# Two trunk layers at fp32: the second and third quarter of the in-projection in one written order

## The chip, the cores and the metric

The kernel runs on one core of a Trainium2 chip. The metric is the device time of one execution in microseconds (us). An execution has one launch; all weights are read from the chip's memory (HBM) once, some 613 MB in all. Five engines work side by side, each in its own order of instructions: TensorE (PE, with its weight loads shown as PEld), VectorE (DVE), ScalarE (ACT), GpSimd (POOL) and SyncE (SP), whose queue issues the transfers. They wait for each other by semaphores.

## What is computed

One inference step of a trunk of two layers with model width 2048, for two groups of requests: 128 context tokens and 128 latent tokens. Everything is float32. Layer 0 mixes with latent attention and grouped-query attention side by side (one combined in-projection of 2048 x 2880, one out-projection), layer 1 with differential attention; each is followed by a gated feed-forward part with a width-3 convolution. Each of these four sub-layers has an adaptive norm:

```python
mod = jax.nn.silu(cond) @ w_ada[l] + b_ada[l]
sh1, sc1, gt1, sh2, sc2, gt2 = jnp.split(mod[:, None, :], 6, axis=-1)
h = rmsnorm(x, g_norm_mix[l]) * (1 + sc1) + sh1
...
proj = h @ w_in
...
x = x + gt1 * m
```

`cond` is one vector for the context group and one for the latent group, so `silu(cond) @ w_ada` is a product with two rows over a 2048 x 12288 matrix for each layer: some 200 MB of weights for very little arithmetic. These weights are a third of the traffic, and the kernel spreads their work over all stages.

## The kernel before

**Layout.** Features lie on the partitions, and both groups of tokens side by side as 256 columns. A matrix product in fp32 is made of three in the type fp32r: weights and activations are each split into a high and a low part, and `wh·xh`, `wh·xl`, `wl·xh` are summed. `split` (lines 243 to 245) does it: a cast on ScalarE writes the high part, a subtraction on VectorE the low part, which therefore comes later. All products go through the helper at line 104, all transposes through the one at line 107, so in the profile they are told apart by tiles: `acc` are the sums of the big products, `ada` those of the adaptive norm.

**Weights** (class `Weights`). A `raw` tile of 1 MB holds 16 blocks of 128 x 128; there are three such buffers, loaded by SyncE's queue (line 291). Its blocks are split eight at a time (1024 columns) into `wh` and `wl`, of which there are four buffers each. `ahead` splits one half of a tile ahead of its use, in pieces of 512 columns, and can be told to pin these instructions. `gemm` makes one output chunk of 128 features; sums have three buffers (`pacc`), and the next chunk can start while an earlier one is still read out.

**Order.** The program is written in one stream, and a planner orders each engine's instructions by a simulated timeline. Instructions handed to `keep_order` keep the program's order among each other on their engine. The object `pe` hands every TensorE instruction to it while `pe.in_turn` is set; before the change that was used in layer 1's mixer alone.

**The adaptive norm's rows.** Units of `w_ada` (layer, one of six parts j, quarter q of the features) are worked off in the order of the list `ROWS`. A unit is four tiles of 1 MB (`row_step`, load at line 534; `araw` with two buffers, for the first units every other tile in the weights' `raw` buffers). `sum_rows` multiplies each tile with `condw`, in four products. `ada_finish` then copies the sums to `am` on ScalarE (line 408), transposes them on TensorE and writes `mod` on VectorE (lines 424 and 426). The first quarter of layer 0 is cut into two halves (`load_half`, `half_unit`, line 359 and lines 363 to 379), so that the first products can start early. `ensure` runs a unit's remaining steps at once; `pump`, called after each chunk, runs as many steps as the stage's rate says.

Some units have no TensorE work for the rows: VectorE sums them in blocks of 256 KB (`side_step`, `sum_block`). A block is loaded at line 497 (three buffers) and takes two instructions at line 478 or 481, one per group, which are pinned. `SIDE` says how many blocks go with one chunk in each stage. A unit has 16 blocks and ends like the others, with a sum over partitions, a copy into `am` and a turn. Three such units (`BESIDE[0]`) belong to layer 0, six to layer 1. Their pool is `beside` in layer 0 and the mixer's own in layer 1. What follows in the pool's place has to wait until the blocks are done, among it `condb` (line 440), a load that lies on SyncE's queue near the end of layer 0's out-projection.

**The in-projection of layer 0** (`mixer_ab`). It is cut along the input features, because the adaptive norm's values come quarter by quarter. `modulate` (lines 591 to 606) makes `hx` for the chunks of a quarter: VectorE and ScalarE scale and shift, ScalarE casts the high part (606), VectorE or GpSimd subtract the low part. `part` then runs 23 output chunks over the quarter's input features: `act.copy` (843) writes the sum for the first part, `dve.tensor_tensor` (845) adds it for the others.

- First quarter: two halves of two input blocks each (6 products per chunk). Beside the first half lie the loads and sums of the second pair of half units (`second_half`).
- Second to fourth quarter: four input blocks each (12 products per chunk). Before each, `ensure` finishes that quarter's two units (scale and shift), then `modulate` runs, then `part`.
- With the fourth quarter `pinned[0]` is set, the caches are loaded, and the blocks on VectorE start (`side_start`). The finishing work of the columns (norms, rotary) runs beside it.

After that come the heads (`head_ab`; softmax weights `p`, line 713), the out-projection with 16 chunks of 48 products and the residual add on VectorE (line 656), and the feed-forward part.

Of the kernel before, what the change touches and what calls it, by code (L numbers as in the profile page):

```python
# [17 lines left out]
P = 128  # L18
D = 2048
KD = D // P  # L20
# [60 lines left out]
FLIMIT = {"ab": 0, "ffn0": 12, "c": 12, "ffn1": 15}  # L81

BESIDE = {0: [17, 18, 19], 1: [26, 27, 28, 29, 30, 31]}
SIDE = {"in3": 0.6, "heads": 1.05, "out0": 0.9, "c": 1.7, "outc": 2.0}
INV = {2048: 0, 768: 1, 512: 2, 128: 3, 256: 4}


# [1 line left out]
def step_kernel(ctx: ExitStack, tc: tile.TileContext, A: dict):  # L89
# [299 lines left out]
    def ada_finish(l, j, q, on_dve, acc=None):  # L389

        got = ada if not on_dve else dict(ada)
        if acc is not None:
            got["acc"] = acc
        home = bank if acc is not None else lambda: T_(ppool["ada"], [P, 512], "ada", bufs=1)

        def reduce():
            ps = home()
            for c in range(2):
                for h in range(2):
                    g = 2 * c + h  # L400
                    pe.matmul(ps[32 * g:32 * g + 32, :NT], C("pick"), got["acc"][c][:, h * NT:(h + 1) * NT],
                              start=True, stop=True, skip_group_check=True)
            got["ps"] = ps

        def copy():
            n = NT if on_dve else 512
            am = T_(tmp, [P, 512], "am", bufs=1)
            act.copy(am[:, :n], got["ps"][:, :n])
            got["am"] = am

        def turn(pin=None):
            pt = bank() if pin else home()
            pin = pin or (lambda i: i)
            for b in range(2 if on_dve else 4):
                pin(pe.transpose(pt[:, b * P:(b + 1) * P], got["am"][:, b * P:(b + 1) * P], ident))
            out = mod[:, l, j, 4 * q:4 * q + 4]
            bias = vector("bada", l, j, q)
            if on_dve:
                two = lambda v: v.rearrange("p (h b) c -> p b c h", b=2)
                dve.tensor_tensor(  # L420
                    out=two(out), in1=two(bias), op=ALU.add,
                    in0=pt[:, :NT].rearrange("p (b c h r) -> p b c h r", b=2, c=2, h=2)[:, :, :, :, 0])
            else:
                dve.tensor_reduce(out=out, in_=pt.rearrange("p (b g r) -> p b r g", b=4, g=4)[:, :, 0:2],
                                  axis=AX.X, op=ALU.add)
# [44 lines left out]
                keep_order(i)  # L470


    side = {"units": [], "k": 0, "due": 0.0, "rate": 0.0, "then": [], "apart": False}

    def sum_block(acc, block, k):
        for c in range(2):
            if k == 0:
                i = dve.tensor_scalar(out=acc[c], in0=block, scalar1=condw[:, k, c:c + 1],
                                      scalar2=None, op0=ALU.mult)
            else:  # L480
                i = dve.scalar_tensor_tensor(out=acc[c], in0=block, scalar=condw[:, k, c:c + 1],  # L481
                                             in1=acc[c], op0=ALU.mult, op1=ALU.add)
            keep_order(i)

    def side_step():
        if side["then"] and not side["apart"]:
# [6 lines left out]
        if k == 0:  # L493
            acc = T_(side["pool"], [P, 2, 512], "aacc", bufs=2 if side["apart"] else 1)
            side["acc"] = [acc[:, 0], acc[:, 1]]
        block = T_(side["pool"], [P, 512], "block", bufs=3)
        sp.dma_start(out=block, in_=A["w_ada"][u[0], u[1], u[2], k // 4][:, k % 4])
        sum_block(side["acc"], block, k)
        side["k"] = (k + 1) % KD
        if k == KD - 1:  # L500
            wait = [lambda: None] * 2 if side["apart"] else []
# [2 lines left out]

    def side_start(name, units, pool_, apart=False):

        side.update(units=[ROWS[u] for u in units], pool=pool_, rate=SIDE[name], due=0.0, apart=apart)

    def side_pump():
        if side["apart"] and side["then"]:  # L510
# [215 lines left out]
    def mixer_ab(hx, rb0, st, beside):  # L726
        l = 0
        with tc.tile_pool(name="ab", bufs=1) as ab:
            with tc.tile_pool(name="abp", bufs=1) as pj:
# [104 lines left out]
                    elif c == 15:  # L834
                        start(values(1))

                def part(W, k0, n, first, rate, between=None, **kw):

                    for c in range(23):
                        ps = gemm(W.chunk(), lambda k: hx[:, k0 + k, :NT], lambda k: hx[:, k0 + k, NT:2 * NT])  # L840
# [4 lines left out]
                            dve.tensor_tensor(out=to, in0=to, in1=ps, op=ALU.add)  # L845
                        if between:
                            between(c)
                        pump(rate, **kw)

                second = {}  # L850
# [10 lines left out]
                        pump(RATE["in0"], until=4)  # L861

                for h in range(2):
                    modulate(hx, rb0, 0, 0, range(2 * h, 2 * h + 2))
                    W = Weights(A["w_in_ab"][3 * h:3 * h + 3], 2, 8, cycle=23)
                    if h == 0:
                        part(W, 0, 2, True, 0, second_half)
                    else:
                        part(W, 2, 2, False, RATE["in0"], until=4)
                W = Weights(A["w_in_ab"][6:], 4, 4, cycle=23)  # L870
                for q in range(1, 4):
                    ensure(0, 1, [q])
# [483 lines left out]
```

## Time and profile before

| | |
|---|---|
| median of 3 runs | 2364.98 us (2364.43 to 2365.27) |
| profiled execution | 2362.85 us |
| its span (first to last instruction) | 2361.1 us |
| mean granted TensorE clock | 0.993 |
| moved by DMA | 612.96 MB, mean 260 GB/s |

The stretches that the change reaches, and what lies around them (bounds rounded to the stage's edges; busy time in us):

| us | stage | PE | DVE | ACT | granted clock | GB/s |
|---|---|---|---|---|---|---|
| 0 to 24 | first loads, first two half units | 9.11 | 8.52 | 9.39 | 1.00 | 366 |
| 24 to 60 | first quarter | 31.25 | 14.81 | 17.66 | 0.91 | 370 |
| 60 to 165 | second and third quarter | 99.78 | 60.10 | 33.66 | 0.98 | 334 |
| 165 to 240 | fourth quarter | 74.05 | 71.91 | 44.98 | 1.00 | 297 |
| 240 to 366 | heads | 124.17 | 88.02 | 63.56 | 1.00 | 308 |
| 366 to 460 | out-projection | 90.98 | 64.03 | 39.28 | 1.00 | 291 |
| 460 to 1160 | feed-forward of layer 0 | 697.16 | 641.91 | 357.12 | 1.00 | 267 |
| 1160 to 2361 | layer 1 | 1180.22 | 898.50 | 598.80 | 0.99 | 233 |

How such rows are read: an engine's busy time is the sum of its instructions' times, and register, branch and DMA-issuing instructions aren't counted. The granted clock is the TensorE clock that the throttle allowed, as a share of full speed. In the timelines quoted below a row gives the time from the span's start, the busy time, the engine, the line, the operation, the output and input tiles, the shapes and how many instructions the row groups; in square brackets stands how long the engine had waited before and for what. In rows of waits, the total, the number of waits and the longest follow the colon.

### The profile page before, as it was taken

What the parts mean: (1) busy time and instruction counts of PE and PEld (TensorE: products, weight loads), DVE (VectorE), ACT (ScalarE), POOL (GpSimd) and SP (SyncE); (2) the same over time, 40 slices, a digit from 0 to 9 for tenths busy, and PEclk for the clock granted to TensorE, in tenths of its full rate; (3) what the DMA queues carried; (4) which work ended last, traced back from release to release, by engine and by line L of the source; (5) the groups of instructions that cost most, each with busy time, mean ns of one, the idle gap of its engine ahead of it and who ended that gap; (6) DMA issues with size and microseconds to landing.
All of it is one profiled execution on the core that took longest, in us unless ns stands there. A gap on an engine that the chain in (4) does not pass through costs nothing. (4 is left out here: it accounts for less than half of the span.)

```text
span 2361.1 us, 47623 instructions
## 1 busy us (share of the span) xinstructions
PE 2306.7 (98%) x19624; PEld 2183.2 (92%) x19624; DVE 1847.8 (78%) x2822; ACT 1164.5 (49%) x1857; POOL 175.7 (7%) x210
## 2 busy tenths in 40 slices
PE   6999999999999999999999999999999999999997
PEld 4778768899999999999989999998999999999997
DVE  3569866779999999999878888798899755666654
ACT  4245544465553355554464444446555534555543
POOL 0002202100000000001220000022000000000011
PEclk9999999999999999999999999999999999999999
DMA  9988888667777877777768888777677555555553
GB/s 368 360 310 283 310 316 328 248 241 251 261 265 285 303 268 260 262 259 274 285 249 279 306 295 312 249 242 271 245 260 258 198 194 197 197 195 191 192 193 124
DMA packets 108249, 612.96 MB, mean 260 GB/s; under 512 B 11712, under 2 KB 19584, under 8 KB 40832
## 3 DMA queue, kind: packets, MB, share of 16 engines
q1 hardware_dynamic: 108032, 609.92, 71.3%
q8 instruction: 154, 2.52, 0.4%
q14 instruction: 63, 0.52, 0.1%
HBM read 605.12 MB, written 4.75 MB: 258 GB/s over the span
## 5 line engine op out<-in xcount | busy, mean ns | idle before, releaser
L104 PE MATMUL acc<-hx,wh 128*128 128x256 f32 x8416 | 1456.3, 278 | 9.3 <-ACT hx L606 4.4
L104 PEld LDWEIGHTS acc<-hx,wh 128*128 128x128 f32 x8416 | 1272.6, 188 | 46.8 <-issue 16.6
L244 ACT CAST wh<-raw 128x1024 fp32r<-128x1024 f32 (+1 forms) x822 | 795.3, 978 | 943.1 <-PE acc L104 759.7
L245 DVE TENSOR_TENSOR wl<-raw,wh 128x1024 fp32r<-128x1024 f32 (+1 forms) x822 | 923.8, 1141 | 315.6 <-ACT wh L244 310.4
L104 PE MATMUL acc<-hx,wl 128*128 128x256 f32 x4208 | 1167.6, 278 | 2.5 <-DVE wl L245 2.3
L104 PEld LDWEIGHTS acc<-hx,wl 128*128 128x128 f32 x4208 | 790.7, 188 | 20.1 <-issue 7.1
L104 PE MATMUL acc<-g,wh 128*128 128x256 f32 x2816 | 478.8, 276 | 0.0
L104 PEld LDWEIGHTS acc<-g,wh 128*128 128x128 f32 x2816 | 423.4, 188 | 0.0
L104 PE MATMUL acc<-g,wl 128*128 128x256 f32 x1408 | 388.0, 276 | 0.0
L452 DVE CUSTOM_DVE_ANT_0 junk<-araw,condb 128x2048 f32<-128x2048 f32 x120 | 274.7, 2289 | 0.0
L104 PEld LDWEIGHTS acc<-g,wl 128*128 128x128 f32 x1408 | 264.2, 188 | 0.0
L481 DVE SCALAR_TENSOR_TENSOR aacc<-block,condw,aacc 128x512 f32<-128x512 f32 x270 | 199.0, 769 | 9.3 <-DMA block<-w_ada 9.0
L200 POOL TENSOR_TENSOR sqacc<-sqacc,sq 128x256 f32<-128x256 f32 x62 | 91.3, 1472 | 1507.6 <-issue 1210.6
L1127 ACT ACTIVATE cv<-acc,convw 128x256 f32<-128x256 f32 x176 | 98.2, 558 | 5.1 <-PE acc L104 5.1
L104 PE MATMUL acc<-oall,wh 128*128 128x256 f32 x512 | 90.3, 281 | 1.8 <-DVE oall L245 1.1
L104 PE MATMUL ada<-araw,condw 128*32 128x512 f32 (+1 forms) x608 | 77.4, 591 | 13.6 <-DMA araw<-w_ada 13.0
L656 DVE SCALAR_TENSOR_TENSOR x<-acc,mod,x 128x128 f32<-128x128 f32 x192 | 58.1, 343 | 39.6 <-PE acc L104 39.6
L1130 DVE SCALAR_TENSOR_TENSOR cv<-acc,convw,cv 128x254 f32<-128x254 f32 x176 | 83.6, 475 | 6.1 <-ACT cv L1127 6.1
L1133 DVE SCALAR_TENSOR_TENSOR cv<-acc,convw,cv 128x254 f32<-128x254 f32 x176 | 84.4, 479 | 3.6
L104 PEld LDWEIGHTS acc<-oall,wh 128*128 128x128 f32 x512 | 78.4, 191 | 2.7 <-DVE oall L245 1.3
L104 PE MATMUL acc<-oall,wl 128*128 128x256 f32 x256 | 71.4, 280 | 0.0
L196 ACT ACTIVATE sq<-x 128x256 f32<-128x256 f32 x75 | 31.0, 415 | 36.2 <-DVE x L656 32.4
(194 smaller groups left out, 1273.7 us busy)
## 6 DMA issues: line engine op xcount, KB each, us to landing
raw<-w_up SPq DMA_DIRECT2D x176, 1024.0 KB, 4.8
araw<-w_ada SPq DMA_DIRECT2D x142, 1024.0 KB, 5.8
raw<-w_down SPq DMA_DIRECT2D x88, 1024.0 KB, 4.8
raw<-w_in_c SPq DMA_DIRECT2D x48, 1024.0 KB, 6.6
block<-w_ada SPq DMA_DIRECT2D x144, 256.0 KB, 5.2
raw<-w_in_ab SPq DMA_DIRECT2D x19, 1024.0 KB, 6.1
raw<-w_out_ab SPq DMA_DIRECT2D x16, 1024.0 KB, 7.4
raw<-w_out_c SPq DMA_DIRECT2D x16, 1024.0 KB, 6.9
```

The costliest lines, as they stand in the source:

```text
L104: return self.placed(nc.tensor.matmul(*a, **kw))
L196: act.activation(sq, src, AF.Square)
L200: eng.tensor_tensor(out=st["acc"], in0=st["acc"], in1=sq, op=ALU.add)
L244: pin(act.copy(out_hi, src))
L245: pin(dve.tensor_tensor(out=out_lo, in0=src, in1=out_hi.bitcast(F32), op=ALU.subtract))
L452: keep_order(dve.tensor_tensor_reduce(out=T_(feat["pool"], [P, D], "junk"), in1=feat["row"][:, c], in0=feat["raw"].rearrange("p g n -> p ( ...
L481: i = dve.scalar_tensor_tensor(out=acc[c], in0=block, scalar=condw[:, k, c:c + 1], in1=acc[c], op0=ALU.mult, op1=ALU.add)
L656: dve.scalar_tensor_tensor(out=x[:, c, s], in0=ps[:, s], scalar=mod[:, l, 3 * which + 2, c, g:g + 1], in1=x[:, c, s], op0=ALU.mult, op1=AL ...
L1127: pin(act.activation(y, ps, AF.Identity, scale=cw[:, 1, m:m + 1], bias=cw[:, 3, m:m + 1]))
L1130: pin(dve.scalar_tensor_tensor(out=y3[:, :, 1:], in0=p3[:, :, :T - 1], scalar=cw[:, 0, m:m + 1], in1=y3[:, :, 1:], op0=ALU.mult, op1=ALU.add))
L1133: pin(dve.scalar_tensor_tensor(out=y3[:, :, :T - 1], in0=p3[:, :, 1:], scalar=cw[:, 2, m:m + 1], in1=y3[:, :, :T - 1], op0=ALU.mult, op1=A ...
```

## The change

It has four parts.

1. **The first weights.** In `mixer_ab` the weights of each half of the first quarter are set up ahead of `modulate`, and for the first half `W.ahead(keep_order)` is called there: the first 8 blocks' splits are made in pieces of 512 columns, pinned. On ScalarE they so stand behind the pinned or earlier instructions of the program, the copy `am` of the second half unit among them.
2. **The blocks' loads.** `side_load` loads a block; `side_start` calls it twice with its issue pinned, and `side_step` then always loads two blocks ahead of the one it sums. As the loads are pinned on SyncE, the planner can't put the first of them at the program's start.
3. **The second and third quarter.** A function `rows(q)` finishes a quarter's two units and modulates. It is called for the second quarter ahead of the loop, and for the third and fourth inside `part`, after chunk 18 of 23 (counted from 0) of the quarter before, through the new argument `then`. During the second and third quarter `pe.in_turn` is set: TensorE's instructions keep the order in which they are written. In the fourth quarter it isn't.
4. **The rates.** `SIDE` rises from 0.6 to 0.7 blocks per chunk in the fourth quarter, from 1.05 to 1.15 in the heads, from 0.9 to 1.1 in the out-projection and from 1.7 to 1.9 in layer 1's mixer. The copy that ends a unit of blocks gets a tile of its own, `amside`, in the blocks' pool.

```diff
-SIDE = {"in3": 0.6, "heads": 1.05, "out0": 0.9, "c": 1.7, "outc": 2.0}
+SIDE = {"in3": 0.7, "heads": 1.15, "out0": 1.1, "c": 1.9, "outc": 2.0}
...
         def copy():
             n = NT if on_dve else 512
-            am = T_(tmp, [P, 512], "am", bufs=1)
+            if acc is None:
+                am = T_(tmp, [P, 512], "am", bufs=1)
+            else:
+                am = T_(side["pool"], [P, NT], "amside", bufs=1)
             act.copy(am[:, :n], got["ps"][:, :n])
...
+    def side_load(pin=lambda i: i):
+        n, k = divmod(side["at"], KD)
+        if n < len(side["all"]):
+            u = side["all"][n]
+            block = T_(side["pool"], [P, 512], "block", bufs=3)
+            pin(sp.dma_start(out=block, in_=A["w_ada"][u[0], u[1], u[2], k // 4][:, k % 4]))
+            side["ahead"].append(block)
+            side["at"] += 1
...
-        block = T_(side["pool"], [P, 512], "block", bufs=3)
-        sp.dma_start(out=block, in_=A["w_ada"][u[0], u[1], u[2], k // 4][:, k % 4])
-        sum_block(side["acc"], block, k)
+        side_load()
+        sum_block(side["acc"], side["ahead"].pop(0), k)
...
+        for _ in range(2):
+            side_load(keep_order)
...
-                def part(W, k0, n, first, rate, between=None, **kw):
+                def part(W, k0, n, first, rate, between=None, then=None, **kw):
...
                         if between:
                             between(c)
+                        if c == 18 and then:
+                            then()
                         pump(rate, **kw)
...
                 for h in range(2):
+                    W = Weights(A["w_in_ab"][3 * h:3 * h + 3], 2, 8, cycle=23)
+                    if h == 0:
+                        W.ahead(keep_order)
                     modulate(hx, rb0, 0, 0, range(2 * h, 2 * h + 2))
-                    W = Weights(A["w_in_ab"][3 * h:3 * h + 3], 2, 8, cycle=23)
...
                 W = Weights(A["w_in_ab"][6:], 4, 4, cycle=23)
-                for q in range(1, 4):
+
+                def rows(q):
                     ensure(0, 1, [q])
                     ensure(0, 0, [q])
-                    pinned[0] = q == 3
-                    if q == 3:
+                    modulate(hx, rb0, 0, 0, range(4 * q, 4 * q + 4))
+
+                rows(1)
+                for q in range(1, 4):
+                    pe.in_turn = q < 3
+                    if q < 3:
+                        part(W, 4 * q, 4, False, RATE["in"], then=lambda: rows(q + 1), until=2 * (q + 2))
+                    else:
+                        pinned[0] = True
                         caches()
                         side_start("in3", BESIDE[0], beside)
-                    modulate(hx, rb0, 0, 0, range(4 * q, 4 * q + 4))
-                    if q < 3:
-                        part(W, 4 * q, 4, False, RATE["in"], until=2 * (q + 2))
-                    else:
                         part(W, 4 * q, 4, False, RATE["in3"], finish)
```

More of the change, by code (lines that the diff above doesn't have):

```diff
@@ L470, in sum_rows @@
                 keep_order(i)
-    side = {"units": [], "k": 0, "due": 0.0, "rate": 0.0, "then": [], "apart": False}
+    side = {"units": [], "k": 0, "due": 0.0, "rate": 0.0, "then": [], "apart": False, "ahead": [], "at": 0}
     def sum_block(acc, block, k):
@@ L505, in side_start @@
     def side_start(name, units, pool_, apart=False):
-        side.update(units=[ROWS[u] for u in units], pool=pool_, rate=SIDE[name], due=0.0, apart=apart)
+        side.update(units=[ROWS[u] for u in units], all=[ROWS[u] for u in units], at=0, pool=pool_,
+                    rate=SIDE[name], due=0.0, apart=apart)
+        for _ in range(2):
+            side_load(keep_order)
     def side_pump():
```

## The prediction

> **What bounds the kernel now.** I read the page first (engines' busy share and the slices), then the stretches, then who TensorE (PE) waits for in each stretch, then the rows around those waits.
>
> ```profile
> span 2361.1 us, 47623 instructions
> PE 2306.7 (98%) x19624; PEld 2183.2 (92%) x19624; DVE 1847.8 (78%) x2822; ACT 1164.5 (49%) x1857; POOL 175.7 (7%) x210
> PE   6999999999999999999999999999999999999997
> DVE  3569866779999999999878888798899755666654
> ```
> ```profile
> 60.00:100.00 40.00, 37.44 (x292) 28.95 (x288) 24.01 (x51) 11.40 (x18) 1.69 (x2) 0.96 0.89 355
> 100.00:165.00 65.00, 62.34 (x491) 48.34 (x488) 36.10 (x67) 22.26 (x30) 2.14 (x2) 1.00 0.85 321
> 165.00:240.00 75.00, 74.05 (x594) 67.00 (x597) 71.91 (x152) 44.98 (x92) 15.91 (x17) 1.00 0.84 297
> 440.00:490.00 50.00, 44.27 (x357) 37.80 (x357) 33.36 (x80) 28.86 (x65) 10.59 (x12) 0.97 0.63 236
> 520.00:560.00 40.00, 40.00 (x356) 40.00 (x355) 37.20 (x48) 21.95 (x31) 0.00 (x0) 1.00 0.71 247
> ```
>
> Each stretch row gives its length, then busy time and count of PE, PEld, DVE, ACT, POOL, the granted clock, DMA share and GB/s. PE bounds everything but the first slice. In 520 to 560 us it runs products alone: 356 in 40.00 us, 0.112 us each; a chunk of 12 products (second to fourth quarter) takes 1.36 us, a chunk of 48 in the out-projection 5.4 us. The multiset of TensorE instructions is the same in both programs, so only PE's idle time and half-clock time can be won, in the stretches that the change reaches. VectorE (DVE) is full in 165 to 240 (71.91 of 75 us): there a second bound lies close.
>
> **The start (first weights behind the second unit's copy; blocks loaded later).**
>
> ```profile
> 6.09 0.33 SPq L291 DMA_DIRECT2D raw<-w_in_ab  x1
> 7.87 2.85 SPq L497 DMA_DIRECT2D block<-w_ada  x3
> 14.97 4.00 SPq L359 DMA_DIRECT2D araw<-w_ada  x2
> 22.83 1.99 ACT L244 CAST wh<-raw 128x1024 fp32r<-128x1024 f32 x2 [3.80 <-DMA raw<-w_in_ab]
> 24.72 0.36 ACT L369 COPY am<-ada 128x256 f32<-128x256 f32 x1
> 26.58 0.88 ACT L605 ACTIVATE nt<-nt,mod,scl 128x128 f32<-128x128 f32 x2 [1.50 <-DVE mod L377]
> 27.36 0.70 ACT L606 CAST hx<-nt 128x256 fp32r<-128x256 f32 x2
> 25.14 0.44 PE L107 MATMUL ada<-cst,am 128*128 128x128 f32 x2 [1.88 <-ACT am L369]
> 27.81 1.01 PE L104 MATMUL acc<-hx,wh 128*128 128x256 f32 x3 [2.23 <-ACT hx L606]
> 28.75 1.94 PE L104 MATMUL ada<-araw,condw 128*32 128x256 f32 x16
> ```
> ```profile
> 23.97:27.38 3.41, 0.44 (x2) 0.20 (x2) 3.15 (x6) 1.92 (x5) 0.00 (x0) 1.00 1.03 424
> 27.38:30.79 3.41, 2.98 (x20) 1.49 (x21) 1.26 (x3) 0.68 (x3) 0.73 (x1) 0.50 1.02 432
> 30.79:34.21 3.42, 3.42 (x19) 3.20 (x23) 0.00 (x0) 0.84 (x2) 0.00 (x0) 0.50 1.01 416
> 75.17:78.58 3.41, 1.61 (x11) 1.17 (x11) 2.80 (x8) 3.41 (x8) 0.00 (x0) 1.00 1.01 416
> 78.58:82.00 3.42, 3.42 (x16) 2.60 (x20) 3.07 (x7) 2.72 (x5) 1.69 (x2) 0.50 0.96 352
> ```
>
> The copy `am` stands behind two weight casts, which waited for their load; so PE's transposes wait 1.88 us and the first products 2.23 us. Behind the copy, the casts become four of 512 columns. ACT then runs: copy at about 23.3 (the unit's products end there), casts to 25.5, `nt` to 26.4, first `hx` at 26.8; 1.0 us sooner than 27.81. DVE's first split now follows the transposes' sum; its price of half a `wl` is hidden, since `nt` on ACT is later.
>
> The queue of DMAs is full here (share 1.03). The three blocks are 786 KB, at 424 GB/s 1.9 us; moved to the fourth quarter, each later load of the start is that much sooner. PE's new order puts the first tile of the next unit (the x16 row, 1.94 us) ahead of the first products. That tile lands some 2.5 us (1 MB at 424 GB/s) after the weights' 22.8, so about 25.5 to 26. PE's unbroken run starts at about 26 in place of 27.81: 1.8 us of work at half clock, 0.9 us at full.
>
> The clock is the larger part. It is 0.50 from 27.38 to 34.21, two windows of 3.41 us; the first had PE busy for 2.98 us and was followed by a second at half, the second was full (3.42) and was followed by full clock. With work from 26 on, the window from 27.38 would be full, and the clock back at 30.79: another 3.41/2 = 1.7 us. I take 0.9 + 1.7 = -2.6. Ends: -0.9 (two windows again), -4.3 (the clock doesn't fall at all).
>
> The Trainium skill ("TensorE: Matmul & The Clock Gate", section "What's actually happening") has full clock after one busy window of about 3.4 us, the windows running free of the kernel. By that the sum is the -2.6 above; the row of 27.38 to 30.79, nearly busy and without effect, speaks for -0.9. The page's free-running windows also mean that the phase is not this change's to set.
>
> **The second half of the first quarter.**
>
> ```profile
> PE acc L104 <- ACT hx L606: 3.4, 2, 2.2
> ```
>
> Of these 3.4 us (20 to 60 us; total, times, longest) the longest is the 2.23 above; the other 1.2 us is at the second half. In the new order two row sums of the next unit stand ahead of its first products, and the transposes stand one chunk earlier. Two sums cost 2 x 0.9 us (rows at 91.31 and 92.19 below) and have to be done anyway, so they fill that hole. -1.2; ends -1.4 and -0.3.
>
> **Second and third quarter in written order.**
>
> ```profile
> PE acc L104 <- DVE wl L245: 2.3, 3, 1.5
> PE ada L107 <- ACT am L408: 2.2, 3, 0.8
> PE ada L104 <- DVE mod L424: 0.6, 2, 0.3
> ```
> ```profile
> 91.31 1.06 PE L104 MATMUL ada<-raw,condw 128*32 128x512 f32 x8
> 92.19 1.04 PE L104 MATMUL ada<-araw,condw 128*32 128x512 f32 x8
> 91.42 0.42 DVE L845 TENSOR_TENSOR proj<-proj,acc 128x256 f32<-128x256 f32 x1 [0.94 <-PE acc L104]
> 91.76 2.36 DVE L245 TENSOR_TENSOR wl<-raw,wh 128x1024 fp32r<-128x1024 f32 x2
> ```
>
> These are all of PE's waits in 60 to 176 us but one of 0.3. The written order puts a chunk (1.36 us) between a unit's last sum and its transposes, and another ahead of the next sum: of the 2.2 us two waits go (1.5; the third, ahead of the second quarter, stays as it is), the 0.6 goes. `rows(q + 1)` after chunk 18 leaves four chunks (5.4 us) beside the modulation; of the 2.3 us the 1.5 (ahead of the second quarter) stays and 0.8 goes. Together -2.9.
>
> Late next: `wl`. The old order starts three chunks on their high parts at a tile's edge, the written one needs the first low part after two products. DVE splits the next tile behind the add of the last chunk (rows at 91.42 and 91.76): first half at 91.76 + 1.18 = 92.94. With one sum between (0.97), PE asks at 91.31 + 0.97 + 2 x 0.11 = 92.5: 0.45 us short. In DVE's new order the split stands so at five of the eleven edges, at the others ahead of that add: +2.2. So -0.7; ends -2.9 (no shortage) and +2.1 (all eleven). The waits of SyncE's queue I followed through: each row tile's buffer frees at least 4 us more than a load's time ahead of its sum, so the fixed order waits for no DMA.
>
> The bubble of 73 to 79 us ahead of the second quarter is unchanged in order (sum, copy, transposes, splits), and so is its half-clock window: 0.
>
> **More blocks per chunk.**
>
> ```profile
> L481 DVE SCALAR_TENSOR_TENSOR aacc<-block,condw,aacc 128x512 f32<-128x512 f32 x26 | 19.2, 763 | 0.7 <-DMA block<-w_ada 0.7
> PE att L107 <- DVE p L713: 1.8, 3, 0.9
> ```
> ```profile
> 456.18 2.18 ACT L244 CAST wh<-raw 128x512 fp32r<-128x512 f32 x4 [4.74 <-DMA raw<-w_up]
> 456.83 0.69 DVE L245 TENSOR_TENSOR wl<-raw,wh 128x512 fp32r<-128x512 f32 x1 [4.90 <-ACT wh L244]
> 457.44 0.60 DVE L656 SCALAR_TENSOR_TENSOR x<-acc,mod,x 128x128 f32<-128x128 f32 x2
> 444.52 0.33 SPq L440 DMA_DIRECT2D condb<-condb  x1
> PE att L104 <- ACT sq L196: 2.9, 1, 2.9
> 1188.94 0.61 DVE L656 SCALAR_TENSOR_TENSOR x<-acc,mod,x 128x128 f32<-128x128 f32 x2 [0.84 <-PE acc L104]
> ```
>
> A block is two instructions of 0.763 us (the group of 165 to 240). In DVE's order nine instead of seven stand ahead of the fourth quarter's last add: +3.1 us on a full engine, against some 2.4 us of modulation that leaves this stretch. PE: +0.4; ends 0 and +3. In the heads 42 instead of 37 are done by the end; DVE has room there, but in its last part PE waits three times for softmax weights (1.8 us), and five more blocks (7.6 us) now lie among them: +0.8; ends -0.5 and +3.
>
> At the end of the out-projection the last residual (457.44) waits on DVE behind a split whose weights came late: their load stands on SyncE behind `condb` (444.52), 2 MB that waits for the blocks' memory. The blocks now end after chunk 6, `condb` goes out at chunk 7, and the residual can follow PE's last product at once, as in the row at 1188.94. Of PE's 2.9 us I take -1.2; ends -2 and 0. `condb` now stands ahead of the weights of chunk 12 on SyncE: 7 us of transfer at 297 GB/s, with four chunks (22 us) in hand, so nothing; without that cover up to 7. `amside` takes the shared copy buffer off the blocks' path, at no cost beyond that memory. Loading two blocks ahead moves no work; a pinned load queues weights behind it on SyncE, within buffers of three as before. In layer 1 (rate 1.9) PE has no DVE wait of this kind in the quoted views; I cost it at 0, ends -1 and +1.5.
>
> **Sum.** -2.6 - 1.2 - 0.7 + 0.4 + 0.8 - 1.2 = -4.5 us. The profiled execution took 2362.85 us (span 2361.1), 2.1 below the median of 2364.98: 2358.4 for such an execution, 2360.5 for the median.
>
> **Rivals.**
> - Larger: the clock falls neither at 27 nor at 79 us (the second window costs 3.42/2 = 1.7). PE was busy 1.61 of 3.41 us ahead of that half clock; a shift of the windows' phase splits that hole over two. -4.5 - 1.7 - 1.7 = -7.9: 2357.1. For it: the windows' phase moves against the work; against: both holes remain.
> - Eaten: the clock needs both windows (+1.7) and six more edges are short of `wl` (+2.7): -0.1, 2364.9. For it: the 27.38 row; against: DVE's order at those edges.
> - Slower: DVE, full from 165 to 240, falls behind by the whole 3.1 us of blocks and carries the lag into the heads' waits, +3 and +3 in place of +0.4 and +0.8, with the clock as before (+1.7): +2.0; where every chunk's add is late by half a block (23 x 0.4), +9. It decides once the adds lag by three chunks (4 us), as PE has three accumulators. About 2370. For it: 71.91 of 75 us; against: the modulation that leaves, and blocks that the queue lets slip behind other work.
>
> **Chances.** Forecast 0.40 (its own range 2358 to 2363), larger 0.24, eaten 0.20, slower 0.16. A change of 0.2% (4.7 us) is about what a measurement of this kernel tells from none. The forecast lies on that edge: 0.22 of its 0.40 below it, with the larger case and a little of the others 0.48 faster; 0.33 within; 0.19 slower. The range takes the larger case's tail (-4.3 at the start, -2.9 in the quarters) and part of the slower: 2353 to 2368.
>
> **What would show it.** Right: first x16 row sum near 26 us, ahead of products; half clock over by 31; in 60 to 165 us only one wait for `am`, and `wl` waits of 0.3 to 0.5, about five; the last residual of the out-projection within 0.2 us of PE's last product. Wrong: half clock to 34; `wl` waits at all edges; PE waits for adds or `wl` in 165 to 240; longer waits for `p` near 350.

## The result, and the profile after

The changed kernel is slower by 0.2%: a median of 2368.25 us over 20 runs (2364.13 to 2375.09) against 2364.40 us over 20 runs of before (2362.53 to 2367.30), ratio 1.002 (95% interval 1.0012 to 1.0028). The forecast was 2360.5, with a range of 2353 to 2368. The profiled execution took 2372.05 us (span 2370.2), 3.8 above its own median; that of before lies 1.6 below the median of these 20 runs. So the two traces show 9.2 us of difference where the runs show 3.85. Executions some 20 to 30 us above all others of the same kernel, of the kernel before too (17 of 159), are left out of every median below, and counts say how many runs are left; in e1, e10 (6 of 12 each) and g1 (5 of 12) they were so many more than in the runs of before beside them (1 of 25, 8 of 35, 3 of 23) that a tendency of a version to them isn't ruled out.

The page of the changed kernel: first the span, then each engine's busy time (share of the span, count of instructions).

```profile
span 2370.2 us, 47635 instructions
PE 2312.7 (98%) x19624; PEld 2188.5 (92%) x19624; DVE 1847.6 (78%) x2824; ACT 1167.2 (49%) x1859; POOL 169.3 (7%) x210
```

Where the time went is told best by counting. Every kernel here issues the same 18,024 big products on TensorE, so the start of the n-th product in two traces can be compared. The table gives the start in the trace of before, and how far the other traces are ahead (-) or behind (+) there, in us. "Old rates" is the changed kernel with the old `SIDE` (the second run of it), "blocks alone" and "new rates alone" are the kernel before with that part of the change; they are told below.

| product | stage that begins | before | changed | old rates | blocks alone | new rates alone |
|---|---|---|---|---|---|---|
| 276 | second quarter | 85.50 | -3.19 | -2.88 | -2.93 | -1.00 |
| 828 | fourth quarter | 174.73 | -3.61 | -2.30 | -5.04 | -0.44 |
| 1104 | heads | 214.23 | -1.56 | -0.51 | -3.11 | +1.20 |
| 1600 | out-projection, just begun | 366.67 | +5.95 | -3.37 | -5.91 | +8.09 |
| 2600 | feed-forward, begun | 506.93 | +5.99 | -5.04 | -7.63 | +6.45 |
| 12400 | last feed-forward, begun | 1709.73 | +8.65 | -4.11 | -5.61 | +6.31 |

The changed kernel leads by 3.6 us where the fourth quarter begins, loses 2.0 in it and 7.5 in the heads, and 2.7 more in layer 1. The heads are where the sign turns. TensorE's waits there, 240 to 366 us, first of before and then of the changed kernel (total, times, longest):

```profile
PE att L107 <- DVE p L713: 1.8, 3, 0.9
```
```profile
PE ada L104 <- DVE mod L427: 3.0, 2, 1.8
PE att L107 <- DVE p L727: 2.3, 2, 1.7
PE ada L104 <- DMA araw<-w_ada: 2.1, 2, 1.5
```

Two kinds of wait are new. The first shows how the row units of TensorE and the blocks of VectorE get into each other's way. The timeline of the changed kernel from 281 us, VectorE's rows and TensorE's:

```profile
281.24 1.23 DVE L245 TENSOR_TENSOR wl<-raw,wh 128x1024 fp32r<-128x1024 f32 x1
282.39 0.29 DVE L687 TENSOR_TENSOR qb<-qb,cst 128x128 f32<-128x128 f32 x1
282.59 1.41 DVE L484 SCALAR_TENSOR_TENSOR aacc<-block,condw,aacc 128x512 f32<-128x512 f32 x2
283.91 0.19 DVE L427 TENSOR_REDUCE mod<-ada 128x8 f32<-128x32 f32 x1
```
```profile
281.05 0.60 PE L107 MATMUL ada<-cst,am 128*128 128x128 f32 x4
281.48 0.83 PE L104 MATMUL att<-pT,vm 128*128 128x128 f32 x6
284.15 1.92 PE L104 MATMUL ada<-araw,condw 128*32 128x512 f32 x16 [1.84 <-DVE mod L427]
```

A unit's transposes end at 281.65. VectorE reads them (L427) only at 283.91, behind a split and a block's two instructions, though its share is 37 of 50 us there. The next unit's sums go to the same bank `ada`, of which there is one, and stand only 0.83 us of other work behind. The same place in the kernel before:

```profile
279.62 0.60 PE L107 MATMUL ada<-cst,am 128*128 128x128 f32 x4
...
281.41 0.18 DVE L424 TENSOR_REDUCE mod<-ada 128x8 f32<-128x32 f32 x1
...
284.65 0.64 PE L104 MATMUL ada<-araw,condw 128*32 128x512 f32 x4
```

There VectorE's read came 1.2 us after the transposes, here 2.3; but above all TensorE's order had 4.4 us of products in between (280.22 to 284.65), and nothing waited. The second stall, 60 us on, drags a load behind it (rows of VectorE, TensorE and SyncE of the changed kernel):

```profile
344.86 0.18 DVE L427 TENSOR_REDUCE mod<-ada 128x8 f32<-128x32 f32 x1
345.10 1.06 PE L104 MATMUL ada<-araw,condw 128*32 128x512 f32 x8 [1.20 <-DVE mod L427]
346.22 0.33 SPq L548 DMA_DIRECT2D araw<-w_ada  x1
347.61 3.95 SPq L493 DMA_DIRECT2D block<-w_ada  x2
354.60 1.06 PE L104 MATMUL ada<-araw,condw 128*32 128x512 f32 x8 [1.47 <-DMA araw<-w_ada]
358.91 1.93 PE L104 MATMUL ada<-araw,condw 128*32 128x512 f32 x8 [0.67 <-DMA araw<-w_ada]
```

The sum at 345.10 is late, it frees the tile's buffer late, the next tile is issued at 346.22 and TensorE waits for it at 354.60. Such holes can then cost the clock, though not each of them does: the windows of 3.41 us from 280.75 and from 345.60, in which TensorE was busy for 1.57 and 1.73 us, were followed by full clock, the one from 352.43, with 1.94, by half clock. Stretches of the changed kernel (length, busy PE, PEld, DVE, ACT, POOL with counts, granted clock, DMA share, GB/s): at the heads' end and at the feed-forward's start:

```profile
355.84:362.67 6.83, 6.16 (x29) 4.19 (x28) 4.03 (x8) 2.63 (x8) 0.00 (x0) 0.50 0.70 251
465.07:475.31 10.24, 9.09 (x41) 6.50 (x38) 8.48 (x25) 6.35 (x17) 3.26 (x5) 0.50 0.85 303
```

Before had full clock at the first place and one window of 3.41 us at the second: (6.83 + 10.24 - 3.41)/2, so by an estimate up to 6.8 us of the 9.2 between the two traces come in this form.

### The profile page after: what moved, and what is told of

The parts are those of the page before. It is cut to its first block, busy times and chain, and to the rows that moved or that the text cites. A ratio compares the mean times of both kernels' runs of the same rounds, so it can differ in the third digit from the quotient of the medians.

```text
span 2370.2 us, 47635 instructions
## 1 busy us (share of the span) xinstructions
PE 2312.7 (98%) x19624; PEld 2188.5 (92%) x19624; DVE 1847.6 (78%) x2824; ACT 1167.2 (49%) x1859; POOL 169.3 (7%) x210
## 5 line engine op out<-in xcount | busy, mean ns | idle before, releaser
L244 ACT CAST wh<-raw 128x1024 fp32r<-128x1024 f32 (+2 forms) x824 | 797.0, 978 | 971.7 <-PE acc L104 778.6
L245 DVE TENSOR_TENSOR wl<-raw,wh 128x1024 fp32r<-128x1024 f32 (+2 forms) x824 | 923.4, 1138 | 312.7 <-ACT wh L244 298.7
L484 DVE SCALAR_TENSOR_TENSOR aacc<-block,condw,aacc 128x512 f32<-128x512 f32 x270 | 197.6, 765 | 10.3 <-DMA block<-w_ada 10.1
L200 POOL TENSOR_TENSOR sqacc<-sqacc,sq 128x256 f32<-128x256 f32 x62 | 85.6, 1381 | 1508.7 <-issue 1211.6
```

The lines of the kernel that those rows point to most:

```text
L200: eng.tensor_tensor(out=st["acc"], in0=st["acc"], in1=sq, op=ALU.add)
L244: pin(act.copy(out_hi, src))
L245: pin(dve.tensor_tensor(out=out_lo, in0=src, in1=out_hi.bitcast(F32), op=ALU.subtract))
```

## The experiments

The first theory after the result: **the rates**. More blocks per chunk put more of VectorE's pinned work ahead of short operations for which TensorE waits. Its rivals: **the lookahead** (blocks' loads ahead of the row tiles on SyncE's queue) and **the clock** (any new order only shifts where half-clock windows fall). Each median below is held against runs of before on the same chip in the same minutes; the intervals (95%) are worked out by drawing anew from both sets of runs.

| run | edit, against | runs left | median | minus before | 95% |
|---|---|---|---|---|---|
| changed kernel | | 20 of 20 | 2368.2 | +3.8 | +2.3 to +7.8 |
| e1 old rates | changed | 6 of 12 | 2358.1 | -6.1 | -9.0 to -5.1 |
| e5 old rates again | changed | 6 of 6 | 2356.4 | -7.4 | -8.7 to -5.2 |
| e2 start and order | before | 10 of 11 | 2363.7 | -0.5 | -1.7 to +1.2 |
| e3 new rates alone | before | 5 of 5 | 2373.5 | +9.3 | +5.0 to +10.5 |
| e4 no lookahead | changed | 7 of 7 | 2370.4 | +6.2 | +5.4 to +8.0 |
| e6 heads' rate old | changed | 11 of 11 | 2363.3 | -0.5 | -1.6 to +3.5 |
| e9 heads' rate alone new | old rates | 9 of 12 | 2362.3 | -2.2 | -4.4 to -1.4 |
| e10 fourth quarter's alone new | old rates | 6 of 12 | 2367.0 | +2.5 | -1.0 to +4.2 |
| e7 layer 1's alone new | old rates | 4 of 4 | 2353.3 | -10.4 | -11.6 to -7.2 |
| f1 the same again | old rates | 12 of 12 | 2356.3 | -8.4 | -9.6 to -6.4 |
| e11 out-projection's and layer 1's new | old rates | 12 of 12 | 2357.3 | -7.2 | -8.1 to -6.0 |
| f4 layer 1's alone new | before | 12 of 12 | 2360.5 | -4.1 | -6.0 to -1.6 |
| e12 turn in another bank | changed | 12 of 12 | 2363.1 | -1.3 | -3.5 to +0.3 |
| f2 the same | f1 | 12 of 12 | 2363.2 | -1.4 | -2.9 to +0.5 |
| e8 planner's order | old rates | 8 of 8 | 2357.9 | -5.9 | -7.3 to -4.9 |
| f3 no part 3 | old rates | 11 of 12 | 2357.8 | -6.8 | -9.6 to -5.3 |
| g1 blocks alone | before | 7 of 12 | 2357.8 | -6.9 | -7.6 to -5.8 |
| g2 first loads not pinned | f3 | 10 of 12 | 2363.0 | -1.7 | -3.3 to -0.4 |

**The rates, taken out and put in alone.**

```diff
-SIDE = {"in3": 0.7, "heads": 1.15, "out0": 1.1, "c": 1.9, "outc": 2.0}
+SIDE = {"in3": 0.6, "heads": 1.05, "out0": 0.9, "c": 1.7, "outc": 2.0}   # e1, e5
```

> The changed kernel with the old rates of blocks (0.6, 1.05, 0.9, 1.7). In the changed kernel's profile the lead over before is 3.6 us at the fourth quarter's start; 2.05 us are lost in that quarter, 7.5 near the heads' end, 2.65 in layer 1. Rates theory (more blocks per chunk on VectorE make those losses): the losses go, about 2361 us, 3 to 4 below before. Lookahead theory (block loads issued two blocks ahead stand before the row tiles on SyncE's queue): the losses stay, about 2368. Clock theory (the planner's new order only shifts where the half-clock windows fall): no pattern, 2364 to 2368.

e3 is the kernel before with the new `SIDE` and `amside`:

> The kernel before with the new rates and the own copy tile alone. Rates theory: slower than before by the losses of the fourth quarter, the heads and layer 1, up to 2 + 7 + 2.6 us: 2370 to 2376, with longer waits for softmax weights or row sums between 340 and 366 us. Lookahead theory: within 2 us of before, 2363 to 2367. Clock theory: 2363 to 2368.

Without the rates the change is a gain of 6 to 7 us; the rates alone are a loss of 9.3. Waits of TensorE from 240 to 366 us, e5 and then e3:

```profile
PE ada L107 <- ACT am L411: 0.3, 1, 0.3
PE att L107 <- DVE p L727: 0.2, 1, 0.2
```
```profile
PE ada L104 <- DMA araw<-w_ada: 3.2, 2, 1.9
PE ada L104 <- DVE mod L427: 2.9, 2, 2.5
PE att L107 <- DVE p L716: 1.9, 2, 1.3
```

The same three waits as in the changed kernel come with the rates on the old program, and go with them on the new one. The clock theory falls (it wanted no pattern).

**The loads ahead, and the start with the order.** e4 leaves out the two calls of `side_load` in `side_start`; e2 is the kernel before with the new text of `mixer_ab` (parts 1 and 3) alone.

```diff
-        for _ in range(2):
-            side_load(keep_order)          # e4
```

> The changed kernel, but each block's load is issued just ahead of its own sum in the program, with the new rates. Lookahead theory: row tiles land in time again, no wait of TensorE for a row tile between 340 and 366 us: about 2361 to 2363. Rates theory: as the changed kernel, about 2368. Clock theory: 2364 to 2368.

> The kernel before with the new start and the written order of the second and third quarter, but without the loads ahead, the own copy tile and the new rates. Both the rates theory and the lookahead theory: the lead of 3.6 us at the fourth quarter stays to the end, less what the early blocks' loads cost at the start (1 to 2 us): 2361 to 2363. Clock theory: 2364 to 2368, with half-clock windows at other places behind 240 us.

e4 is no better than the changed kernel. It also gives up the pin of the first two loads, which below turns out to be worth some 5 us, so its time alone doesn't decide; but its trace has more waiting for row tiles in the heads (5.7 us against 2.1), without the lookahead, so the lookahead isn't the cause of these waits. e2 fell between the theories' numbers: its trace leads by 2.5 us at the second quarter's start and by 0.5 at the fourth's, and parts 1 and 3 alone gain nothing that can be told (-0.5). What then makes the 6 to 7 us?

> The changed kernel with all the old rates, a second time. Its first runs fell into two groups, 2355 to 2360 (5) and 2384 to 2388 us (7); one of 25 runs of before (2395) and one of 11 with start and order alone (2394) lay as far above the rest. If the 29 us belong to this kernel's order, both groups come again, about half and half, and the time lies in one place of the trace where that run is profiled; if they belong to the chip in those minutes, the high group is rare now. The low group, by the rates theory, is again 2355 to 2360.

All six runs lie between 2354.8 and 2359.2, so the gain came again. (The first twelve were six and six, not five and seven.)

**Which rate.** Each run is the changed kernel with a `SIDE` of its own: e6 has 0.7, 1.05, 1.1, 1.9; e9 has 0.6, 1.15, 0.9, 1.7; e10 has 0.7, 1.05, 0.9, 1.7; e7 and f1 have 0.6, 1.05, 0.9, 1.9; e11 has 0.6, 1.05, 1.1, 1.9.

> The changed kernel with the heads' old rate (1.05) and the other rates new. If the heads' rate makes the heads' loss: the lead of some 1.5 us at the end of the fourth quarter is still there at 366 us, no wait of TensorE for the row units' turn or for row tiles in the heads, and the time is 2360 to 2363 (layer 1's loss stays). If the blocks that the fourth quarter brings ahead are enough: the waits near 284 and 345 us stay, 2366 to 2369.

> The changed kernel with only the heads' rate new (1.15), the others old. The two runs of the old rates gave 2356.4 and, in their low group, 2358.0; with the new rate everywhere but in the heads it was 2363.3. If the heads' rate makes waits of its own (five more blocks among the softmax weights): waits for the row units' turn or for row tiles between 280 and 360 us, 2360 to 2365. If it takes the fourth quarter's rate to make them: none of these waits, 2355 to 2359.

> The changed kernel with only the fourth quarter's rate new (0.7). If its three blocks more, which shift everything that the planner lays out behind them, are the cause of the losses in the heads: waits for the turn near 283 us and for a row tile near 345 us as with the old heads' rate alone, 2361 to 2366. If not: the fourth quarter's own loss alone, 0.5 us, 2356 to 2359.

Against the old rates (-6 to -7), the heads' rate alone costs some 4 to 5 us, the fourth quarter's alone some 9, though that is the median of only six runs. e6, where the heads' rate alone is old, isn't cleared: TensorE waits 2.0 us for the turn and 3.2 for a row tile there. The blocks that VectorE has done near the heads' end (product 1560), counted in the traces, are 37 in before, e1, e5, e11, f3 and g1, 39 in e6, e9 and e10, 42 in the changed kernel, e3 and e4. From product 1104 to 1600 the traces take 149.6 (e5) and 149.6 us (g1) with 37 of them, 155.5 (e9), 153.7 (e10) and 159.0 (e6) with 39, 159.9, 159.3 and 162.6 with 42. Within a group the clock differs (e6 had 13.65 us at half clock in the heads, e10 3.41). With half of the half-clock time taken off, which is an estimate, the three groups lie at 149.6, at 152.0 to 153.8 and at 156.5 to 160.9 us, so the loss grows with the blocks, though there are only two or three traces to a group, and before, with 37 blocks and no pin, takes 152.4. Which wait they make differs with the order. The larger waits of e10 from 240 to 366 us, where the turn and a tile are late, and then those of e9, where it is the softmax weights:

```profile
PE ada L104 <- DMA araw<-w_ada: 3.2, 1, 3.2
PE ada L104 <- DVE mod L427: 1.1, 1, 1.1
```
```profile
PE att L107 <- DVE p L727: 3.9, 2, 2.3
PE ada L104 <- DVE p L727: 1.6, 1, 1.6
```

**Layer 1's rate.**

> The changed kernel with the old rates in layer 0 and the new one (1.9) in layer 1's mixer. If the 2.65 us lost in layer 1 of the changed kernel's profile come from its rate: 2.65 above the low group of the old rates, 2358 to 2363, with the loss near 1290 us again. If they were only where a half-clock window fell: as the old rates, 2355 to 2360.

> The changed kernel with the old rates in the fourth quarter and the heads, and the new ones in the out-projection (1.1) and layer 1 (1.9). The new rate in layer 1 alone gave 2353.3. If the prediction's step on the out-projection (the long load ahead of the weights goes out earlier) needs the new rate there: 1 us less, 2352 to 2353. If the last residual is in time either way: 2352 to 2355. If the out-projection's rate harms: above 2356.

> The changed kernel with the old rates in layer 0 and the new one in layer 1, a second time, with more rounds. The first time it was 10.5 us below before in four runs, three of them at a mean clock of 0.997; with the out-projection's new rate beside it the gain was 7.2 in twelve runs. If the layer's rate is worth 3 us: 10 below before again. If the four runs had a lucky clock: 7 to 8 below before, as the old rates.

> The kernel before with the new rate in layer 1 (1.9 for 1.7) and the own copy tile alone. If the blocks' earlier end frees VectorE at the layer's out-projection, where it is full before: 2 to 3 us below before. If the rate is worth nothing: within 1 us of before. If it loses as in the changed kernel's profile (2.65 us between 1277 and 1303 us): 2 to 3 above.

On the kernel before, together with the own copy tile, it gains 4.1 us (1.6 to 6.0); on the old rates 1 to 4, less clear. The copy tile was not run alone. The loss in the changed kernel's trace, one wait of 1.51 us for softmax weights and a half-clock window at 1297.92 us, isn't the rate's as such: f4's trace has such a wait too (2.0 us), the seven others with that rate (e3, e4, e6, e7, e11, e12, f1) have none. The out-projection's rate shows nothing or a small loss.

**The shared bank.** e12 is the changed kernel, f2 the kernel of f1, each with

```diff
-            pt = bank() if pin else home()
+            pt = bank() if pin or (acc is None and ada.get("apart")) else home()   # set in the heads
```

> The changed kernel with all new rates, where in the heads the transposes of a row unit go to the bank of the small sums instead of the one in which the next unit's rows are summed; the next sum then no longer waits for VectorE to read them. In the changed kernel's profile these waits were 3.0 us, with waits for softmax weights 2.3, for row tiles 2.1, and 6.8 us of half clock. If the turn behind the blocks starts the chain (tiles late because the sums are late): 2360 to 2364. If only the two waits go: 2364 to 2367. If the shared bank of the small sums makes new waits: 2368 or more.

> The same with the row units' transposes in the heads in the bank of the small sums. With the old rates the heads have no wait for the turn, so this can win little: 0 to 1 us below the kernel without it. If the bank's waits for small sums (1.1 us in the run with all new rates) come here too: 1 us above.

In e12 the wait for `mod` is gone and the time falls from 3.8 above before to 1.3 below. In its trace, though, the stretch from product 1104 to 1600 takes 157.4 us, 2.5 less than in the changed kernel and 7.8 more than in e5. And f2, where there was no such wait, loses 7 against f1 and ends at the same 2363. The larger waits from 240 to 366 us, of e12 and then of f2:

```profile
PE att L107 <- DVE p L727: 1.5, 2, 0.9
PE ada L104 <- DMA araw<-w_ada: 1.1, 2, 0.8
PE misc L104 <- DVE rv L208: 1.1, 1, 1.1
```
```profile
PE ada L104 <- DMA araw<-w_ada: 1.6, 2, 1.4
PE att L107 <- DVE p L727: 1.6, 3, 0.6
PE acc L104 <- ACT vt L967: 1.1, 1, 1.1
PE acc L104 <- ACT kn L963: 0.7, 1, 0.7
```

Only the 1.1 us of e12 for `misc` is a wait at the shared bank itself. So e12 shows that the bank takes part in the loss, not that it is all of it; and f2 that the other bank, with the order that the planner makes of it, can cost as much as the new rates.

**What gains.** e8 is e1 with `pe.in_turn = False`; f3 is e1 with the kernel before's loop over the quarters (no `rows`, no `then`, no written order); g1 is f3 without `W.ahead(keep_order)`; g2 is f3 with `side_load()` unpinned in `side_start`.

> The changed kernel with all the old rates and without the written order on TensorE (the next quarter's rows still at chunk 18). In the changed kernel's profile the written order gained 0.4 us between the second and the fourth quarter's start, as waits for low parts took most of what the copies' waits gave. By that: 0 to 1 us above the old rates' low group, 2356 to 2361. If the order is worth what the prediction's waits without the shortage say (2.9 us): 2358 to 2363. If the planner does better than the writing: below 2355.

> The changed kernel with all old rates and without part 3: the rows of the next quarter and the modulation follow the quarter before, as in the kernel before, and the planner orders TensorE. With part 3 but the planner's order on TensorE the time was 5.9 us below before, with the written order 6.3 and 7.4. If the start and the later blocks make the gain (2.6 and 1.2 us in the prediction) and part 3 is worth 0.5 to 1: 5 to 6 us below before. If part 3's early modulation is what pays (waits for copies and low parts, up to 2.9 us): 3 to 4 below before.

> The kernel before with the blocks' part alone: the loads two blocks ahead with the first two pinned, and the own copy tile, at the old rates; no first weights ahead, no part 3. With the first weights ahead it was 6.8 us below before, and the first weights with the written order but the blocks loaded early 0.5 below. If the blocks' loads leaving the start, and what follows in the heads and at the out-projection's end, make nearly all of the gain: 5 to 7 below before. If the first weights behind the copy need them away but earn it themselves (the prediction's start, 2.6 us): 3 to 4 below.

> The start and the blocks' part at the old rates, without part 3, but the first two loads of blocks not pinned, so that three blocks are loaded at the start again, ahead of the second pair of half units. If the place of these loads at the start is what counts: the 3 us at the start go, and the order behind may change, 1 to 4 us below before. If the loads ahead in the heads count alone: 5 to 7 below before.

f3 and g1 settle it: without the written order, and without the first weights too, the whole gain is there (-6.8, -6.9). It hangs on one thing, the pin of two loads (g2: -1.7). In g1's trace 2.9 us are won by the second quarter's start (three blocks fewer ahead of the row tiles: the next unit's first sum stands at 25.89 us, in before at 28.75), 2.1 in that quarter and the third, 1.9 of which the fourth gives back, 2.8 in the heads, where the waits for softmax weights fall from 1.8 us to 0.2, and 1.7 from there to the feed-forward's start, as TensorE's wait at the out-projection's end falls from 2.9 to 1.1. Why the pin clears the heads isn't settled: with 37 blocks in all these traces it is the planner's order that differs. But it does so each time: the eight traces with the pin and with the old rates in the fourth quarter and the heads (without the other bank) take 149.6 to 150.1 us from product 1104 to 1600, the four with these rates and without the pin (before, e2, f4, g2) 152.3 to 152.4.

The written order loses in its own stretch. From product 276 to 828 the three traces with the pin and the planner's order (e8, f3, g1) take 86.6 to 87.1 us, the eleven with the pin and the written order 88.5 to 90.4, and none of them has half clock there. From 84 to 176 us TensorE waits 1.4 us for low parts in e8, 3.1 in e5. In the times of the runs this can't be told (-5.9 to -6.9 against -6.1 and -7.4).

The fastest version is that of e7 and f1: 2356.3 against 2364.6 us (-8.4, -9.6 to -6.4) in twelve runs.

## Why the prediction was wrong, step by step

- **The start, -2.6, and the second half, -1.2:** -3.2 together at the second quarter's start (-2.9 in e5). The first sum of the next unit stood at 25.90, ahead of the products, and full clock was back at 31.57, as said. The clock was luck: half clock lasted one window here, but with the same start two in the traces of e9, e10, e11 and f1 (to 34.5 to 35.2 us), and in those of e6 and e7 no fall is recorded. And the first part of the reason was wrong. The copy came no earlier, and the first product came later (28.35 against 27.81):

```profile
21.00 3.64 PE L104 MATMUL ada<-raw,condw 128*32 128x256 f32 x32 [1.16 <-DVE mod L375]
24.77 0.37 ACT L369 COPY am<-ada 128x256 f32<-128x256 f32 x1 [6.07 <-PE ada L104]
25.90 1.07 PE L104 MATMUL ada<-araw,condw 128*32 128x256 f32 x16 [0.27 <-DVE mod L375]
28.35 1.59 PE L104 MATMUL acc<-hx,wh 128*128 128x256 f32 x4 [1.38 <-ACT hx L620]
```
```profile
21.33 1.93 PE L104 MATMUL ada<-raw,condw 128*32 128x256 f32 x32 [1.17 <-DVE mod L375]
```

  The second fence is before: there the unit's 32 products took 1.93 us, here 3.64. In 18 of the 20 traces of this study they took 3.27 to 3.64, in two 1.93. So the trace of before was the rare case, and in the common one the copy waits for these products and not for the casts. Beside the pinned loads part 1 adds nothing that can be told (g1 against f3). Without the pin it shows at the second quarter's start (-2.5 in e2, -2.1 in g2, against +0.5 in f4, which has neither), but that lead is gone by the fourth (-0.5 and +1.1).
- **The quarters, -0.7:** the lead grew by 0.4. The waits came out as worked: those for `am` fell from 2.2 to 0.8 us, those for `mod` went, those for `wl` rose from 2.3 to 3.8 (seven instead of three; the 0.45 at five edges makes +2.2, less the 0.8 that goes). Over the runs part 3 can't be told from nothing (f3). The bubble at 73 to 79 us, which the text put ahead of the second quarter, lies at the last weight tile of the first quarter's second half; it stayed.
- **The fourth quarter, +0.4:** +2.0, within its ends. Eight blocks were done by its end, not nine, for seven. But e5 and g1 lose 1.8 and 1.9 there at the old rate, so beside the pin the rate adds little; without the pin the new rates alone lose 1.6 (e3). Why the pin costs that much in this quarter isn't shown.
- **The heads, +0.8 with ends -0.5 and +3: the step that failed.** It measured +7.5 in the trace, and 10.3 against e5's heads (159.9 for 149.6). The count was right (42 for 37 blocks). The text priced them as VectorE's room and as delay of the softmax weights, and these waits did grow only from 1.8 to 2.3. What it left out: the turn of a row unit is VectorE's work too, it holds the one `ada` bank, and behind it hang the next sums, the tile's buffer, the next load, and the clock. That is not all of it: e12, without the turn's wait, still takes 157.4, and in e9 it is the softmax weights that are late (3.9 and 1.6 us), the very price that the text put at +0.8. How the loss divides between these waits isn't shown.
- **Loads two blocks ahead, "moves no work":** wrong, with the other sign. The pin is what gains (g1, g2), in the heads too.
- **The out-projection's end, -1.2:** TensorE's wait fell from 2.90 to 1.32 us, and the last residual came with the last product (462.01), as said. The reason isn't the rate: e7, with the old one, has 1.09 there. In the changed kernel's trace the gain went into 10.24 us of half clock: the lag is 5.95 us at the out-projection's start and 5.99 behind its end.

```profile
462.01 0.61 DVE L670 SCALAR_TENSOR_TENSOR x<-acc,mod,x 128x128 f32<-128x128 f32 x2 [0.84 <-PE acc L104]
463.41 0.38 PE L104 MATMUL att<-cst,sq 128*128 128x1 f32 x2 [1.32 <-ACT sq L196]
```

- **Layer 1, 0 with ends -1 and +1.5:** a gain of 4.1 us by f4 (with the copy tile) and 1 by f1 against e5, at or beyond the lower end.

What came was the rival on the other side in outcome (about 2370, chance 0.16), not in mechanism: no lag of the adds in the fourth quarter, but latency in the heads with VectorE three quarters busy. The rival's +9 was worked with 0.4 us for half a block, too; by the text's own 0.763 us for one of a block's two instructions it is 0.76.

## What to carry to other kernels

Work put "beside" on an engine that isn't full still costs, if the instructions are pinned and short operations that the bounding engine waits for stand behind them: price it by what is queued behind each, and follow the resource that the late one holds (here a bank, then a buffer, then a load). Where parts of a change can be run singly, run them so before reading the sum: here a part costed at nothing made the whole gain, and the part that the change is named for made none that the runs show. One trace is one draw of the clock; a hole's price in it can be off by more than the whole change.

## What the runs showed of the hardware that was not expected

- After holes alike in size the half clock lasted from none to three windows. At the feed-forward's start, behind a wait of 1 to 3 us, the traces have 3.41 us (before), 10.24 (changed kernel, e2, e6), 6.83 (f1), 3.41 (e5, g1), none (e7, f3). With half of such a window lost, that alone is 0 to 5.1 us from trace to trace. The Trainium skill ("TensorE: Matmul & The Clock Gate", section "What's actually happening") says that the windows run free of the kernel and that the number of slow products varies by run; the traces agree (the first half-clock window begins at 27.38 us in before, at 28.16 in the changed kernel). The same section of the Trainium skill calls the half clock the state at rest; the 32 products at 21 us, which took 1.7 to 1.9 times as long in 18 of 20 traces as in the other two, fit that, though the clock records of the 18 begin only at 23.9 us or later.
- In the clock records of the 20 traces half clock never began behind a window of 3.41 us in which TensorE was busy for more than 73%. The reverse doesn't hold: behind windows of 44 to 73% it came in some cases and not in others. And five half-clock windows in which TensorE was busy throughout were followed by another one.
- In one execution of e10 products were 4% slower for the last 740 us while the granted clock read 1.00. Stretches of e10 early and late, and of before late:

```profile
700.00:800.00 100.00, 100.00 (x884) 100.00 (x884) 92.22 (x110) 41.35 (x43) 0.00 (x0) 1.00 0.77 283
2150.00:2200.00 50.00, 50.00 (x426) 50.00 (x426) 32.19 (x43) 25.50 (x36) 0.00 (x0) 1.00 0.53 190
```
```profile
2150.00:2200.00 50.00, 50.00 (x443) 50.00 (x442) 34.50 (x47) 26.18 (x37) 0.00 (x0) 1.00 0.56 198
```

  884 products in 100 us are 0.1131 us each, 426 in 50 are 0.1174. From product 11800 (at 1642 us) to 18000 this trace falls evenly behind that of e9, by 27.5 us in all; the stretches of layer 0 that are read above lie ahead of that. By how many products a full stretch holds it can be seen; the clock's rows don't show it, and nothing here says what it comes from.
